# A one-core hybrid decoder layer: products of ones where TensorE waits, a fixed order of the first loads, new FFN shares and leads, one half's sums inside the last down products

## The chip, the cores and the metric

The kernel runs on one core of one Trainium2 chip. The metric is device time in microseconds (us) of one execution. Five engines work side by side, each through its own list of instructions in a fixed order: TensorE (PE in the profile; the load of its stationary operand is a row of its own, PEld), VectorE (DVE), ScalarE (ACT), GpSimd (POOL) and SyncE (SP), which here only starts DMA transfers. An engine that waits for a semaphore holds up everything behind it on its list.

## The reference

One layer for 2056 tokens: a prompt of 2048 and 8 decode tokens. Everything is float32.

```
n  = rmsnorm(x, g1);   [x_branch 512 | gate 512 | q 512 | k 128 | v 128] = n @ w_in
rec = lru(conv4(x_branch)) * gelu(gate)              # per-token scan, block-diagonal gates
att = window_attention(q, k, v, sinks)               # 8 heads, self + 128 tokens back
h  = x + concat(rmsnorm(rec), rmsnorm(att)) @ w_out
h2 = rmsnorm(h, g2);   y = h + (silu(h2 @ w_gate) * (h2 @ w_up)) @ w_down      # 1024 -> 2816 -> 1024
return rmsnorm(y, g_final), the k, v and conv windows, the last LRU states
```

## The kernel before

Tokens lie along the free dimension, features on the 128 partitions. A float32 product is made of a rounded part hi and a remainder lo of each operand: three products, w_hi x_hi, w_hi x_lo and w_lo x_hi, replace each one (`mm3`, issued by `mm`, line 358; transposes by `tr`, line 363). So every weight chunk is loaded raw (`raw_...`, line 344), cast on ACT (line 347) and given a remainder on POOL (line 348), and every activation chunk gets hi on ACT (line 387) and lo on DVE (line 388).

**Head phase, 0 to about 691 us.** Four sub-blocks of 520, 512, 512 and 512 tokens. Per sub-block s: `prep` loads x in 8 chunks (`xs`, line 627), makes hi and lo, and sums squares (ACT line 395 or 398, DVE line 399) into `xacc`; TensorE sums that over the partitions (`st_x`), DVE adds the epsilon (line 409), POOL takes the power -1/2 (line 410), TensorE spreads the result over all partitions (`bc_x`, line 358 as all products), ACT copies it out (`rb_x`, line 426). The 14 input units (`ip<s>_<u>`, 48 products of 260 columns in sub-block 0, 24 of 512 after it) need that factor only when DVE evicts them (line 673). Then follow the recurrence's gates (`g`), attention (`s`, `pt`, `o`), a norm over each group (`st_rc`, `bc_rc`, `st_at`, `bc_at`) and the output units (`op`). In this phase a table, `PE_ORDER`, fixes the order of all products, one token per tile and a count; `order_pe` chains them. The other engines' orders come from a scheduler: each step has a planned due time built from constants (`T_...`, `L_...`, `D_...`, `F_...`), and instructions go out by these. Before sub-block 0 stands a chain of small DVE operations on the parameter vector (lines 585 to 604: `hab`, `hxb`, `nsk`, `sp`, `c2`, `nc2`).

**FFN, about 691 to 2060 us.** Three groups gi of about 688 tokens, two halves n each. For each of 11 pairs p of hidden chunks, gate and up come as seven products of sums and differences of quarters (`ps_g`, `ps_u`, numbered r); ACT copies them out (lines 1337, 1342, 1344), DVE and POOL combine them (lines 1298 to 1316). The down product is either plain (`pd`, 16 tiles, added to `y` on DVE at line 1373) or, for gi 1 and 2 and p 1 to 9, again in seven products (`pw`, added at line 1402). Remainders of the weights are made at line 1131 (gate, up) and line 1200 (`wd`, down). Tables `E_...` say for each of these operations whether POOL ("P") or DVE ("V") does it.

**Tail.** `finish` squares each finished `y` chunk of the last group (ACT, line 398), adds the squares on DVE (line 399), then runs `st_f`, the power, `bc_f` and, per chunk, one DVE operation (line 1424) and one output DMA on SP (line 1427). The last down products do half 1 (8 tiles) and then half 0 (8 tiles); the sums of both halves come behind them.

Of the kernel before, what the change touches and what calls it, by code (L numbers as in the profile page):

```python
# [67 lines left out]
E_T2 = ['V', 'P', 'P', 'P']
E_HN = ['P', 'P', 'P', 'P']
# [33 lines left out]
ip0_1_0 ip0_1_1 ip0_12_0 ip0_12_1 ip0_1_0:2 ip0_1_1:2 ip0_12_0:2 ip0_12_1:2 ip0_1_0 ip0_1_1 ip0_12_0 ip0_12_1  # L103
ip0_1_0:2 ip0_1_1:2 ip0_12_0:2 ip0_12_1:2 ip0_1_0 ip0_1_1 ip0_12_0 ip0_12_1 ip0_1_0:2 ip0_1_1:2 ip0_12_0 ip0_1_0
ip0_1_1 ip0_12_0:2 ip0_12_1:3 ip0_1_0:2 ip0_1_1 ip0_1_0 ip0_1_1:2 ip0_12_0:3 ip0_12_1:3 ip0_1_0:3 ip0_1_1:3 ip0_12_0
ip0_1_0:2 ip0_1_1:2 ip0_12_0 ip0_1_0 ip0_1_1 ip0_12_0:4 ip0_12_1:2 ip0_1_0:3 ip0_1_1:3 ip0_12_0:3 ip0_12_1:4
ip0_1_0:2 ip0_1_1:2 ip0_12_0:2 ip0_12_1:5 ip0_9_0:3 st_x0:5 ip0_9_0:21 ip0_9_1:18 bc_x0_0:4 ip0_9_1:6 ip0_8_0:24
ip0_8_1:4 bc_x0_4 ip0_8_1:20 ip0_0_0:24 ip0_0_1:19 g0_1_0_0 ip0_0_1:5 ip0_3_0:20 g0_1_0_260 ip0_3_0:4 ip0_3_1:12
g0_1_1_0 ip0_3_1:12 ip0_11_0:14 g0_1_1_260 ip0_11_0:10 ip0_11_1:15 vt0_0 ip0_11_1:9 ip0_10_0:23 vt0_1 ip0_10_0
ip0_10_1:24 ip0_13_0:3 vt0_2 ip0_13_0:21 ip0_13_1:6 vt0_3 ip0_13_1:18 ip0_2_0:7 s0_0_0:4 ip0_2_0:5 s0_0_1:4 g0_0_0_0  # L110
ip0_2_0:12 ip0_2_1:6 s0_1_0:4 s0_1_1:4 ip0_2_1:2 g0_0_0_260 ip0_2_1:10 pt0_0_1:4 ip0_2_1:4 s1_0_0:4 ip0_2_1:2
ip0_5_0:3 s1_0_1:4 ip0_5_0 g0_0_1_0 ip0_5_0:9 o0_0_0 ip0_5_0:10 s1_1_0:4 ip0_5_0 o0_0_0 pt0_1_1:4 ip0_5_1:4
g0_0_1_260 ip0_5_1 s1_1_1:4 ip0_5_1:19 ip0_4_0:2 s2_0_0:4 ip0_4_0:7 o0_1_0 ip0_4_0:11 pt1_0_0:4 o0_1_0 ip0_4_0:2
s2_0_1:4 ip0_4_0:2 ip0_4_1:24 ip1_8_0:15 ip0_6_0:9 o1_0_0 ip0_6_0 pt1_0_1 o1_0_0 pt1_0_1:3 ip0_6_0 ip1_8_0 g0_3_0_0
# [3 lines left out]
s3_0_0:4 ip0_7_0:2 o1_1_1:2 s3_0_1:4 bc_x1_0 ip0_7_1:2 bc_x1_0 ip0_7_1:3 pt2_0_0:4 ip0_7_1:19 o2_0_0:2 pt2_0_1:2  # L118
g0_2_0_0 pt2_0_1 ip1_10_0:8 pt2_0_1 ip1_10_0:12 o2_0_1 ip1_10_0 g0_2_0_260 ip1_10_0 s3_1_0:4 pt2_1_0:4 s3_1_1:4
ip1_10_0:2 o2_0_1 ip1_11_0:14 g0_2_1_0 ip1_11_0:10 ip1_4_0:4 o2_1_0 ip1_4_0:2 pt2_1_1 o2_1_0 pt2_1_1:3 g0_2_1_260  # L120
ip1_4_0:18 ip1_0_0:2 o2_1_1 ip1_0_0 vt1_0 ip1_0_0:6 dS:2 o2_1_1 dS:6 pt3_0_0:4 ip1_0_0:12 o3_0_0 ip1_0_0:3
ip1_12_0:2 dS2:2 ip1_12_0:2 pt3_0_1 o3_0_0 ip1_12_0 pt3_0_1:3 ip1_12_0:18 o3_0_1 ip1_12_0 ip1_13_0:4 o3_0_1
pt3_1_0:4 ip1_13_0:9 dS3 ip1_13_0 dS3 ip1_13_0:10 ip1_1_0 o3_1_0 pt3_1_1:3 ip1_1_0:2 pt3_1_1 o3_1_0 ip1_1_0 dS4:4
s4_0_0 dS4:4 ip1_1_0:8 o3_1_1 s4_0_0:3 s4_0_1:4 ip1_1_0:2 o3_1_1 ip1_1_0:10 ip1_5_0:7 dS5:2 s4_1_0:2 s4_1_1:4
ip1_5_0 s4_1_0:2 vt1_1 ip1_5_0:11 pt4_0_0:2 ip1_5_0 pt4_0_0:2 ip1_5_0:4 s5_0_0:4 ip1_2_0 s5_0_1:4 ip1_2_0 vt1_2
ip1_2_0:7 o4_0_0 ip1_2_0:9 pt4_0_1 o4_0_0 pt4_0_1:3 ip1_2_0:3 vt1_3 ip1_2_0:3 o4_0_1 s5_1_0:4 s5_1_1:4 o4_0_1
pt4_1_0:4 st_rc0:5 ip1_6_0:24 pt4_1_1:4 bc_rc0_0:3 s6_0_0:4 bc_rc0_0 s6_0_1:3 pt5_0_0:4 bc_rc0_4 s6_0_1 g1_0_0_0
g1_0_1_0 st_at0:5 ip1_3_0:24 bc_at0_0:4 ip1_7_0:24 op0_0_0:2 bc_at0_4 op0_0_0:10 op0_0_260:12 op0_1_0 g1_1_0_0
op0_1_0:11 op0_0_0 op0_0_260 op0_1_0:4 op0_0_0:6 op0_1_0:3 op0_0_260:9 op0_1_0:3 op0_0_0:3 g1_1_1_0 op0_0_0:2
op0_0_260:2 op0_1_0:2 o4_1_0:2 op0_1_260:4 o4_1_1:2 op0_1_260:20 op0_2_0:11 pt5_0_1:4 op0_2_0:12 o5_0_0:2 op0_2_0  # L130
op0_2_260:13 s6_1_0:4 op0_2_260:3 s6_1_1:4 op0_2_260:2 o5_0_1 op0_2_260:6 op0_3_0:5 o5_0_1 g1_2_0_0 op0_3_0
pt5_1_0:4 op0_3_0:18 op0_3_260:16 g1_2_1_0 op0_3_260:8 op0_4_0:18 o5_1_0 op0_4_0:2 pt5_1_1 o5_1_0 op0_4_0 pt5_1_1:3
op0_4_0:3 op0_4_260:24 op0_5_0 o5_1_1 s7_0_0:4 op0_5_0:4 s7_0_1:4 op0_5_0:8 o5_1_1 pt6_0_0:4 op0_5_0:11 op0_5_260:11
g1_3_0_0 op0_5_260:13 o6_0_0 op0_6_0:3 pt6_0_1 o6_0_0 pt6_0_1:3 op0_6_0:5 g1_3_1_0 op0_6_0:10 o6_0_1 op0_6_0:6
op0_6_260 s7_1_0:4 op0_6_260 s7_1_1:4 op0_6_260 o6_0_1 pt6_1_0:4 op0_6_260:21 op0_7_0:17 o6_1_0 bc_x2_0:3 pt6_1_1
o6_1_0 bc_x2_0 pt6_1_1:3 op0_7_0:7 op0_7_260:17 o6_1_1 op0_7_260:7 ip2_4_0:20 o6_1_1 pt7_0_0:4 ip2_4_0:4 ip2_0_0:8
st_h0:5 ip2_0_0:2 o7_0_0 ip2_0_0:2 o7_0_0 ip2_0_0:6 pt7_0_1:4 ip2_0_0:6 ip2_5_0:2 st_rc1:4 o7_0_1 ip2_5_0:3 o7_0_1
pt7_1_0:4 ip2_5_0:13 bc_rc1_0:4 ip2_5_0:3 o7_1_0 ip2_5_0:3 pt7_1_1:3 ip2_1_0:2 pt7_1_1 o7_1_0 ip2_1_0:8 g2_0_0_0
ip2_1_0:12 o7_1_1 ip2_1_0:2 o7_1_1 g2_0_1_0 ip2_8_0:24 ip2_12_0:18 g2_1_0_0 ip2_12_0:6 ip2_9_0:19 g2_1_1_0 ip2_9_0:5
ip2_10_0:24 ip2_11_0:3 vt2_0 ip2_11_0:21 ip2_2_0:8 vt2_1 ip2_2_0:16 ip2_13_0:6 vt2_2 ip2_13_0:18 ip2_7_0:7 vt2_3  # L140
ip2_7_0:17 ip2_3_0:5 s8_0_0:4 s8_0_1:3 st_at1:4 s8_0_1 ip2_3_0:19 ip2_6_0 s8_1_0:4 s8_1_1 bc_at1_0:4 s8_1_1
# [1425 lines left out]
```

## Time and profile before

| What | Before |
|---|---|
| Runs | 2077.74, 2079.32, 2082.77 us; median 2079.32 us |
| Profiled execution | 2078.05 us, of which the span is 2076.3 us |
| Around the span | 1.75 us |
| Mean granted TensorE clock | 0.994 of full |
| PE / DVE / ACT / POOL busy | 2014.0 / 1440.0 / 939.9 / 929.3 us |
| DMA | 450.96 MB, mean 217 GB/s |

Times in the profile's rows count from the start of the span. In a timeline row stand start, duration, engine, line, operation, output tile and operands, partitions x elements, count; in brackets how long the engine had been idle, and what ended that. A row of windows gives, for a stretch, its length and for each engine its busy time and instructions, then the granted clock (1.00 is full), the DMA share and GB/s. The list of waits gives total, number and longest. A float32 product that is not split leaves two records.

### The profile page before, as it was taken

The page shows a single profiled execution, that of the slowest core. Times are in us where ns is not written, and L with a number is a line of the kernel's source. Part 1 is how long each engine was busy: PE and PEld are TensorE (multiplying, and loading weights), DVE is VectorE, ACT ScalarE, POOL GpSimd, SP SyncE. Part 2 cuts the span into 40 slices and gives each one's busy share as a digit, 9 for nine tenths or more (in the row PEclk, how much of TensorE's full clock was granted, in tenths as well). Part 3 has the DMA queues.
Part 4 walks back from the last instruction along what each step waited for, and adds up shares of the span by engine and source line. Part 5 has one row for each costly group of instructions (what it writes and reads, how often), then busy time and mean ns, then how long its engine had stood idle before and what let it go on. Part 6 is the DMA issues. An engine that isn't in the chain of part 4 may idle for free.

```text
span 2076.3 us, 34690 instructions
## 1 busy us (share of the span) xinstructions
PE 2014.0 (97%) x12238; PEld 1903.0 (92%) x12238; DVE 1440.0 (69%) x2683; ACT 939.9 (45%) x1954; POOL 929.3 (45%) x820
## 2 busy tenths in 40 slices
PE   8999899999999999999999999999999999999997
PEld 8988787878777899999999999999999999999997
DVE  6786896766885755656654578777666666777676
ACT  5764684563554543344334533334335433433342
POOL 5212342020122787667776845455446522433332
PEclk9999999999999999999999999999999999999998
DMA  8864485576677955656555776776677775566652
GB/s 300 264 209 149 165 281 178 189 241 198 205 259 263 332 200 199 211 201 215 189 197 187 253 266 213 244 235 227 217 242 251 241 231 195 183 197 196 195 181 87
DMA packets 208990, 450.96 MB, mean 217 GB/s; under 512 B 25232, under 2 KB 82720, under 8 KB 208800
## 3 DMA queue, kind: packets, MB, share of 16 engines
q1 hardware_dynamic: 205616, 446.24, 64.4%
q10 hardware_dynamic: 3200, 2.51, 0.4%
q8 instruction: 96, 1.57, 0.3%
q14 instruction: 78, 0.64, 0.1%
HBM read 335.89 MB, written 113.84 MB: 217 GB/s over the span
## 4 chain that ended last, share of the span: by engine, by line
PE 69%; DVE 12%; DMA 9%; issue 4%; ACT 3%; POOL 2%; SPq 1%; DVEq 0%; ACTq 0%; POOLq 0%
PE ps_u L358 17%; PE ps_g L358 17%; PE pd L358 10%; PE ip L358 10%; PE pw L358 9%; DMA n<-hs 4%; PE op L358 2%; DMA rd<-in_wdown 1%; DMA xs<-in_xT 1%; DMA mixed<-n 1%; DVE y L1424 1%; DVE xc L696 1%; DVE n L485 1%; DVE n L477 1%; PE o L358 1%
## 5 line engine op out<-in xcount | busy, mean ns | idle before, releaser
L358 PE MATMUL ps_g<-hn,w_g 128*128 128x342 f32 (+1 forms) x2772 | 491.9, 321 | 4.7 <-ACT c_g L1337 2.5
L358 PE MATMUL ps_u<-hn,w_u 128*128 128x342 f32 (+1 forms) x2772 | 482.5, 320 | 0.7 <-ACT c_u L1342 0.7
L358 PEld LDWEIGHTS ps_g<-hn,w_g 128*128 128x128 f32 x2772 | 447.0, 189 | 6.4 <-ACT c_g L1337 2.7
L358 PEld LDWEIGHTS ps_u<-hn,w_u 128*128 128x128 f32 x2772 | 444.3, 189 | 1.6 <-ACT c_u L1342 1.0
L358 PE MATMUL ip<-xn,w_in 128*128 128x512 f32 (+1 forms) x1680 | 354.3, 360 | 11.7 <-ACT xn L387 8.3
L358 PEld LDWEIGHTS ip<-xn,w_in 128*128 128x128 f32 x1680 | 274.2, 192 | 57.1 <-ACT xn L387 8.3
L1402 DVE TENSOR_TENSOR y<-y,pw 128x342 f32<-128x342 f32 x504 | 238.6, 503 | 55.4 <-PE pw L358 54.2
L358 PE MATMUL pd<-fh,w_d 128*128 128x344 f32 (+1 forms) x960 | 238.7, 321 | 1.5 <-DVE y L1373 1.5
L358 PE MATMUL op<-mix,w_out 128*128 128x512 f32 (+1 forms) x960 | 205.1, 359 | 1.5 <-ACT mix L777 1.4
L358 PEld LDWEIGHTS op<-mix,w_out 128*128 128x128 f32 x960 | 156.2, 189 | 30.5 <-issue 5.3
L358 PE MATMUL pw<-fh,wd 128*128 128x342 f32 x576 | 168.2, 321 | 2.5 <-DVE y L1402 2.5
L358 PEld LDWEIGHTS pd<-fh,w_d 128*128 128x128 f32 x960 | 168.2, 188 | 2.1 <-DVE y L1373 1.8
L1373 DVE TENSOR_TENSOR y<-y,pd 128x344 f32<-128x344 f32 (+1 forms) x240 | 117.0, 506 | 70.6 <-PE pd L358 69.1
L1298 POOL TENSOR_TENSOR c_u<-c_u,c_g 128x342 f32<-128x342 f32 (+1 forms) x60 | 63.7, 1062 | 210.3 <-DVE c_u L1316 199.4
L1287 DVE TENSOR_TENSOR fl<-c_u,fh 128x342 fp32r<-128x342 f32 (+1 forms) x132 | 115.6, 882 | 59.9 <-ACT fh L1286 58.4
L358 PE MATMUL pd<-fl,w_d 128*128 128x344 f32 (+1 forms) x480 | 154.0, 321 | 1.6 <-DVE fl L1287 1.6
L1286 ACT CAST fh<-c_u 128x342 fp32r<-128x342 f32 (+1 forms) x132 | 62.5, 479 | 161.1 <-POOL c_u L1298 87.7
L1200 POOL TENSOR_TENSOR wd<-rd,wd 128x512 fp32r<-128x512 f32 x72 | 98.5, 1369 | 77.9 <-ACT wd L1199 75.0
L358 PE MATMUL pw<-t,wd 128*128 128x342 f32 x648 | 125.1, 320 | 3.7 <-DVE y L1402 3.7
L1316 DVE TENSOR_TENSOR c_u<-c_u,ps_u 128x342 f32<-128x342 f32 (+1 forms) x99 | 50.3, 508 | 107.0 <-PE ps_u L358 106.7
L1130 ACT CAST w_u<-ru 128x512 fp32r<-128x512 f32 x99 | 61.3, 620 | 111.0 <-PE pd L358 38.0
L358 PEld LDWEIGHTS pw<-t,wd 128*128 128x128 f32 x648 | 105.8, 189 | 5.3 <-DVE y L1402 4.9
(280 smaller groups left out, 3479.6 us busy)
## 6 DMA issues: line engine op xcount, KB each, us to landing
w_g<-split_g SPq DMA_DIRECT2D x88, 512.0 KB, 4.4
w_u<-split_u SPq DMA_DIRECT2D x88, 512.0 KB, 5.3
w_in<-split_w SPq DMA_DIRECT2D x84, 512.0 KB, 3.8
rg<-in_wgate SPq DMA_DIRECT2D x110, 256.0 KB, 3.3
ru<-in_wup SPq DMA_DIRECT2D x110, 256.0 KB, 3.3
w_out<-split_w SPq DMA_DIRECT2D x48, 512.0 KB, 5.1
split_g<-w_g SPq DMA_DIRECT2D x44, 512.0 KB, 3.6
split_u<-w_u SPq DMA_DIRECT2D x44, 512.0 KB, 3.7
```

Of the source, the lines that this page charges most:

```text
L358: r = nc.tensor.matmul(*args, **kw)
L477: nc.vector.scalar_tensor_tensor(x, x, col(V_G2 + k), bc[n][:, :nn], ALU.mult, ALU.mult)
L485: (nc.gpsimd if M_MIX else nc.vector).tensor_tensor(x, a, b, op=op)
L696: nc.vector.scalar_tensor_tensor(xc[:, :n], xr[:, j:j + n], cw[j], xc[:, :n], ALU.mult, ALU.add)
L1130: nc.scalar.copy(w[:, 0, :], src)
L1200: eng((E_DLO1, E_DLO2)[gi - 1][j]).tensor_tensor(w[:, :, 1], v, w[:, :, 0].bitcast(F32), op=ALU.subtract)
L1286: nc.scalar.copy(hi, v)
L1287: nc.vector.tensor_tensor(lo, v, hi.bitcast(F32), ALU.subtract)
L1298: (nc.vector if p == NPAIR - 1 or src is not v else eng(E_MUL[2 * h + n])).tensor_tensor(v, src, g, op=ALU.mult)
L1316: nc.vector.tensor_tensor(o, a, b, op)
L1373: nc.vector.tensor_tensor(ys[gi, n, m], ys[gi, n, m], ps, ALU.add)
L1402: nc.vector.tensor_tensor(v, v, ps, ALU.add)
```

## The change

It has four parts.

**1. Products of ones.** `PE_ORDER` now also holds tokens `w_<tile>:n`. When that tile is allocated, n products of a 128x128 block of ones with itself go into its first 128 columns; the tile's own first product overwrites them (`start=True`). They wait for whatever the tile's memory waits for, and for nothing else. There are 48: st_x0 9, pt2_0_0 2, bc_rc0_4 1, st_at0 6, o8_0 1, s11_1_1 1, pt15_0_0 1, op3_0_0 4, op3_3_1 1, ps_g0_0_5 13, and in the tail st_f2_0 5 and bc_f2_0 4.

```
+        def filled(ps, name):
+            for _ in range(FILLS["w_" + name]):
+                mm("w_" + name, ps[:, :P], ones, ones, start=True, stop=True)
+            return ps
```

**2. First loads.** `prep(0)` is replaced by `prep_first`, which issues the first weights and x chunks in one list, chains ACT's casts, hi parts and squares in the same order, and chains DVE's lo parts (0 to 7) and square additions (8 + chunk):

```
+FIRST = [(1, 0), 0, (12, 0), 1, 2, 3, (1, 1), 4, 5, (12, 1), 6, 7, -1]
+FIRST_DVE = [0, 1, 9, 2, 3, 10, 4, 5, 6, 7, 11, 12, 13, 14, 15]
```

A pair (u, i) is half i of the weights of unit u, a number an x chunk, -1 the constants `cs`, which ACT's queue loaded before. On SP's queue the first rows were these (`raw_in_u_i` is a weight half, `xs` an x chunk, the last two share a tile):

```order
L344 DMA raw_in_1_0_278<-in_win 128x512
L344 DMA raw_in_1_1_284<-in_win 128x512
L344 DMA raw_in_12_0_290<-in_win 128x512
L627 DMA xs_0_195<-in_xT 128x520
L627 DMA xs_1_202<-in_xT 128x520
L627 DMA xs_2_210<-in_xT 128x520
L627 DMA xs_3_218<-in_xT 128x520
L344 DMA raw_in_12_1_296<-in_win 128x512
```

and now they are:

```order
L351 DMA raw_in_1_0_159<-in_win 128x512
L671 DMA xs_0_162<-in_xT 128x520
L351 DMA raw_in_12_0_164<-in_win 128x512
L671 DMA xs_1_167<-in_xT 128x520
L671 DMA xs_2_169<-in_xT 128x520
L671 DMA xs_3_171<-in_xT 128x520
L351 DMA raw_in_1_1_173<-in_win 128x512
L671 DMA xs_4_176<-in_xT 128x520
```

The first x chunk has moved from fourth to second place. On DVE the 31 small operations of the parameter chain, which stood ahead of the first lo part and among the following ones, now stand behind the last square addition.

**3. Shares, leads, order.** Planner constants and the recorded `PE_ORDER` have new values; for the most part products swap places with a neighbour. Of the shares these change (what moves is counted from the engines' lists):

```
-E_LO0 = ['P', 'V', 'P', 'V', 'P', 'V', 'P']      +E_LO0 = ['V', 'V', 'V', 'V', 'P', 'P', 'P']
-E_LO2 = ['V', 'V', 'V']                          +E_LO2 = ['V', 'V', 'P']
-E_DLO1 = ['P', 'V', 'P', 'V', 'V', 'P', 'V']     +E_DLO1 = ['P', 'P', 'P', 'V', 'P', 'V', 'V']
-E_DLO2 = ['P', 'P', 'P', 'P', 'P', 'P', 'V']     +E_DLO2 = ['V', 'P', 'V', 'P', 'V', 'V', 'P']
-E_T1 = ['P', 'P', 'P', 'V']                      +E_T1 = ['P', 'P', 'P', 'P']
-E_T2 = ['V', 'P', 'P', 'P']                      +E_T2 = ['P', 'V', 'P', 'P']
-E_HN = ['P', 'P', 'P', 'P']                      +E_HN = ['P', 'V', 'P', 'P']
```

Group 0: 22 remainders of gate and up go from POOL to DVE. Group 1: 9 remainders `wd` and 9 combinations `c_u` go from DVE to POOL, 7 `hn` from POOL to DVE. Group 2: 22 remainders of gate and up go from DVE to POOL, 27 `wd` and 7 `hn` from POOL to DVE.

At the start of the FFN, TensorE's list (`ps_g_0_r` is product r of the gate of pair 0; number 6 takes the memory of number 1, number 5 that of an earlier output unit) had

```order
L358 MATMUL ps_g_0_2_7775<-hn_0_4_6445,w_g_0_2_7723 128x344
L358 MATMUL ps_g_0_1_7758<-hn_0_5_6452,w_g_0_6_7738 128x344 x3
L358 MATMUL ps_g_0_1_7758<-hn_0_6_6512,w_g_0_6_7738 128x344 x4
L358 MATMUL ps_g_0_1_7758<-hn_0_7_6532,w_g_0_6_7738 128x344
L358 MATMUL ps_g_0_1_7758<-hn_0_6_6512,w_g_0_6_7738 128x344
L358 MATMUL ps_g_0_1_7758<-hn_0_7_6532,w_g_0_6_7738 128x344 x3
L358 MATMUL ps_g_0_5_7809<-hn_1_0_7638,w_g_0_5_7742 128x344 x4
```

and now has

```order
L384 MATMUL ps_g_0_2_7803<-hn_0_4_6461,w_g_0_2_7751 128x344
L384 MATMUL ps_g_0_5_7837<-ones 128x128 x13
L384 MATMUL ps_g_0_5_7837<-hn_1_0_7666,w_g_0_5_7770 128x344 x4
L384 MATMUL ps_g_0_5_7837<-hn_1_1_7679,w_g_0_5_7770 128x344
L384 MATMUL ps_g_0_5_7837<-hn_1_0_7666,w_g_0_5_7770 128x344
L384 MATMUL ps_g_0_5_7837<-hn_1_1_7679,w_g_0_5_7770 128x344 x3
L384 MATMUL ps_g_0_5_7837<-hn_1_2_7688,w_g_0_5_7770 128x344 x3
L384 MATMUL ps_g_0_1_7786<-hn_0_5_6472,w_g_0_6_7766 128x344 x3
```

Products 5 and 6 have changed places, and 13 products of ones stand ahead of number 5.

**4. Tail.** `finish_last` replaces `finish` for the last group. Half 1's squares are added on DVE (odd chunks) and POOL (even), half 0's on POOL, and half 0's last square is not added but summed by TensorE. Half 1's last DVE operations run from the first on as its factor comes, those from the third on behind half 0's last `y` addition and those from the sixth on behind half 0's epsilon addition. Half 0's output DMAs alternate between SP's and ACT's queue.

```
+F_PLACE = [3, 6]
+F_HOLD = [2, 5]
+            for place, r in zip(F_PLACE, ends):
+                for m in range(place, KD):
+                    behind(tail_pd[m], r)
```

Behind the last down product (`pd_10_7_0`) TensorE's list ended with

```order
L358 MATMUL pd_10_7_0_22494<-fh_10_10_7627,w_d_10_11_22327 128x342
L358 MATMUL st_f_1_22506<-avg,acc_f_1_22346 114x1 x3
L358 MATMUL st_f_0_22520<-avg,acc_f_0_22434 114x1 x3
L358 MATMUL bc_f_1_0_22512<-cs,cols_f_1_22417 128x114 x3
L358 MATMUL bc_f_0_0_22530<-cs,cols_f_0_22505 128x114 x3
```

and now ends with

```order
L384 MATMUL pd_10_7_0_22548<-fh_10_10_7655,w_d_10_11_22368 128x342
L384 MATMUL st_f_0_22564<-ones 128x128 x5
L384 MATMUL st_f_0_22564<-avg,acc_f_0_7486 114x1
L384 MATMUL st_f_0_22564<-avg,sq_f_0_7_22561 114x1
L384 MATMUL st_f_0_22564<-avg,acc_f_0_7486 114x1
L384 MATMUL st_f_0_22564<-avg,sq_f_0_7_22561 114x1
L384 MATMUL st_f_0_22564<-avg,acc_f_0_7486 114x1
L384 MATMUL st_f_0_22564<-avg,sq_f_0_7_22561 114x1
L384 MATMUL bc_f_0_22578<-ones 128x128 x4
L384 MATMUL bc_f_0_22578<-cs,cols_f_0_22563 128x114 x3
```

Half 1's two groups of small products (`st_f_1`, `bc_f_1`) have left this place; they now stand ahead of tiles 3 and 6 (counted from 0) of half 0's eight down tiles.

More of the change, by code (lines that the diff above doesn't have):

```diff
@@ L108 @@
[L108 to L112, printed above, removed]
```

433 lines of the change are left out of this document (272 added, 161 removed).

## The prediction

> **What bounds the kernel now.** I read the page first, then the waits of TensorE, then windows of 3.41 us, then the timelines of the start and the end. On the page TensorE is busy nearly throughout:
>
> ```profile
> PE 2014.0 (97%) x12238; PEld 1903.0 (92%) x12238; DVE 1440.0 (69%) x2683; ACT 939.9 (45%) x1954; POOL 929.3 (45%) x820
> ```
>
> So the time is the sum of TensorE's products plus what it loses in between: 2076.3 - 2014.0 = 62 us idle, and some products at a lower clock. The change adds 48 products and removes none, so whatever it gains comes out of these losses. The waits of TensorE name them (total, number, longest):
>
> ```profile
> PE ip L358 <- ACT xn L387: 8.3, 1, 8.3
> PE pw L358 <- DVE y L1402: 6.3, 8, 1.9
> ...
> PE st_at L358 <- ACT ia L711: 1.7, 1, 1.7
> ...
> PE op L358 <- ACT mix L777: 1.4, 1, 1.4
> ```
>
> The largest is the first: 8.3 us until the first product can run. The rest are small and many. The clock is the second kind of loss. It sits at half only in single stretches; these windows show them, the loss ahead and, for two, the half clock behind it:
>
> ```profile
> 217.11:220.53 3.42, 1.89 (x14) 1.69 (x15) 3.39 (x6) 3.21 (x6) 0.00 (x0) 1.00 0.00 0
> 220.53:223.94 3.41, 3.41 (x10) 2.67 (x9) 3.41 (x7) 1.38 (x2) 1.73 (x1) 0.50 0.00 0
> 544.79:548.21 3.42, 1.53 (x7) 0.74 (x5) 3.42 (x13) 2.41 (x8) 2.04 (x3) 1.00 0.45 116
> ...
> 636.95:640.37 3.42, 2.03 (x12) 1.77 (x13) 3.42 (x6) 3.23 (x6) 0.00 (x0) 1.00 0.75 260
> ...
> 694.98:698.39 3.41, 0.96 (x6) 0.88 (x6) 3.38 (x6) 2.24 (x5) 2.83 (x2) 1.00 0.99 324
> 698.39:701.81 3.42, 3.42 (x14) 3.42 (x13) 3.42 (x4) 1.90 (x2) 2.65 (x3) 0.50 1.05 403
> ...
> 1507.34:1510.76 3.42, 1.60 (x10) 1.60 (x11) 2.65 (x7) 0.00 (x0) 0.00 (x0) 1.00 1.03 394
> ```
>
> Where TensorE was busy for 0.96 to 2.03 us of a window, the clock (third number from the end) was 0.50 in the next one (220.53 and 698.39 show it); the window of 1.60 at 1507 was followed by none, so the bound isn't sharp. Each drop costs up to half of 3.41 us, 1.7 us. A product of ones therefore has a purpose where it lifts a window above the bound, and a price where it stands behind the wait.
>
> **Price of a product of ones.** It isn't in the trace. The nearest rows are the broadcasts of one 128x128 float32 block:
>
> ```profile
> 634.51 1.16 PE L358 MATMUL bc_rc<-cs,rccols 128*128 128x128 f32 x8 [0.34 <-POOL rccols L410]
> 635.43 0.47 PE L358 MATMUL o<-pth,vt 128*128 128x512 f32 x1
> ```
>
> Eight records are four products; from 634.51 to the next start they took 0.92 us, so 0.23 us each at full clock, 0.46 at half.
>
> **Start.** Up to the norm's sums (`st_x`) everything hangs on the first loads and on DVE:
>
> ```profile
> 8.26 1.24 PE L358 MATMUL ip<-xn,w_in 128*128 128x260 f32 x4 [8.26 <-ACT xn L387]
> ...
> 24.69 1.08 PE L358 MATMUL st_x<-avg,xacc 128*104 128x1 f32 x10
> ```
> ```profile
> 4.12 0.62 ACT L347 CAST w_in<-raw_in 128x512 fp32r<-128x512 f32 x1 [0.96 <-DMA raw_in<-in_win]
> 7.48 0.73 ACT L387 ACTIVATE xn<-xs,vec 128x520 fp32r<-128x520 f32 x1 [0.16 <-DMA xs<-in_xT]
> ```
> ```profile
> 16.45 1.30 POOL L348 TENSOR_TENSOR w_in<-raw_in,w_in 128x512 fp32r<-128x512 f32 x1 [2.63 <-DMA split_w<-w_in]
> 16.47 1.31 DVE L599 TENSOR_SCALAR sp<-sp 128x4 f32<-128x4 f32 x1
> 21.21 0.75 DVE L388 SCALAR_TENSOR_TENSOR xn<-xs,vec,xn 128x520 fp32r<-128x520 f32 x1
> 21.88 0.21 DVE L698 SCALAR_TENSOR_TENSOR xc<-scv,vec,xc 128x8 f32<-128x8 f32 x1
> 22.02 0.15 DVE L603 TENSOR_SCALAR c<-sp 128x4 f32<-128x4 f32 x1
> 23.95 0.69 DVE L399 TENSOR_TENSOR xacc<-xacc,sq_x 128x520 f32<-128x520 f32 x1
> 31.98 0.43 DVE L673 TENSOR_TENSOR xr<-ip,rb_x 128x260 f32<-128x260 f32 x1 [6.01 <-ACT rb_x L426]
> ```
>
> The first weight landed at 4.12, the first x chunk, three loads later, at about 7.4: 1.1 us a load. Second in the queue it lands near 5.2, its hi part takes 0.73, so the first product runs at about 5.9 instead of 8.26. From there DVE decides. It makes eight lo parts (0.75 each, 6.0 us) and seven additions (0.69 each, 4.8); and it stands still while POOL makes a weight remainder, as the pair at 16.45 and 16.47 shows (1.31 us for an operation that takes 0.15 otherwise). Four such remainders fall into this stretch, 1.2 us each, 4.8 us. That is 15.6 us, less the 0.08 us by which one starts before the one ahead ends (0.75 at 21.21, the next at 21.88) at each of 15, about 14.5; from 5.9 the last addition ends near 20.5 instead of 24.64. So `st_x` comes 4.2 us earlier. The 96 products ahead of it have by then been issued either way. The nine products of ones (4.1 us at half clock) lie in the time when TensorE waits for the first load and cost nothing there.
>
> What is late next: the 31 small DVE operations, now behind the last addition. At 0.15 each they need 4.7 us, and the idle time they move into is 6.01 us, ahead of the first eviction. POOL's remainders may stretch them by 1 to 2 us beyond it, and TensorE itself then stands about 2.5 us ahead of `st_x`, long enough for a drop. I take 0.7 us off: **3.5 us gained, bounds 5.5 and 1.0**.
>
> **Head phase after it.** At 640 the four products of ones (0.9 us) lie in the 1.4 us wait of `op`, so they cost nothing and lift that window to 2.9: 1.7 gained. At 218 the six stand behind the release that `st_at` waits for (1.7 us) and cost 1.4 us; the drop they prevent costs 1.7: 0.3 gained. At 548 no product of ones stands near; the order there changes a little, and I take 0.6 of the possible 1.7. The swaps of neighbours in the order I can't price; the nearest rows are the single waits above, 1.4 to 1.9 us, so two of them either way. **2.6 gained, bounds 6 gained and 3 lost.**
>
> **Start of the FFN.**
>
> ```profile
> 691.14 3.92 PE L358 MATMUL ps_g<-hn,w_g 128*128 128x344 f32 x24
> 697.52 5.59 PE L358 MATMUL ps_g<-hn,w_g 128*128 128x344 f32 x24 [2.45 <-ACT c_g L1337]
> ```
>
> The second 24 products waited for ACT's copy of product 1, whose memory product 6 takes, and then ran half cold: 5.59 against 3.92, 1.67 us lost. Now product 5 comes first, whose memory is free; but 13 products of ones (3.0 us) stand ahead, from 695.06 to 698.05, so real work starts 0.5 us later, at full clock. Ahead of them nothing queues on TensorE that could have gone; behind them the whole list. **1.2 gained; bounds 2.5 gained, or 1.5 lost** if the second half's `hn`, which ACT and DVE make just then, isn't ready at 698.
>
> **Shares in the FFN.**
>
> ```profile
> 1138.00:1582.00 444.00, 435.08 (x2761) 430.86 (x2761) 317.73 (x564) 168.94 (x352) 237.05 (x218) 1.00 0.70 235
> 1595.00:2025.00 430.00, 429.09 (x2738) 428.51 (x2737) 303.47 (x541) 168.07 (x349) 162.81 (x140) 1.00 0.64 206
> 691.00:1120.00 429.00, 422.32 (x2666) 420.04 (x2665) 255.77 (x381) 174.88 (x349) 317.83 (x238) 1.00 0.61 209
> ```
> ```profile
> L1200 DVE TENSOR_TENSOR wd<-rd,wd 128x512 fp32r<-128x512 f32 x18 | 17.0, 945 | 0.0
> ...
> L1312 DVE TENSOR_TENSOR c_u<-c_u,c_u 128x342 f32<-128x342 f32 x9 | 5.1, 563 | 0.0
> ```
> ```profile
> L1131 POOL TENSOR_TENSOR w_g<-rg,w_g 128x512 fp32r<-128x512 f32 x21 | 30.3, 1442 | 21.4 <-ACT w_g L1130 18.6 <-DMA sums_d<-sd 1.5 <-issue 1.3
> ...
> L1200 POOL TENSOR_TENSOR wd<-rd,wd 128x512 fp32r<-128x512 f32 x18 | 25.1, 1397 | 22.4 <-ACT wd L1199 22.4
> ```
>
> TensorE idles 444.0 - 435.1 = 8.9 us in group 1, 0.9 in group 2, 6.7 in group 0 (2.45 of it priced above). In group 1 DVE gives away 9 x 0.945 + 9 x 0.563 = 13.6 us and takes seven `hn`, so it falls from 318 to about 311 us of 444. The 6.3 us for late `y` additions are all DVE's; I give a quarter back, 1.5. In group 0 POOL, the fullest engine at 318 of 429, loses 22 x 1.44 = 32 us: 0.5. In group 2 DVE loses 22 remainders and gains 27 `wd` at 0.945 and seven `hn`, about even, and there is nothing to win: 0. **2.0 gained, bounds 8 gained and 6 lost** (all idle time of groups 0 and 1 above gone by half, or group 2 taking on group 1's 6.3).
>
> **Tail.**
>
> ```profile
> 2060.03 0.51 DVE L1373 TENSOR_TENSOR y<-y,pd 128x342 f32<-128x342 f32 x1
> ...
> 2060.64 0.49 ACT L398 ACTIVATE sq_f<-y 128x342 f32<-128x342 f32 x1 [0.45 <-DVE y L1373]
> ...
> 2061.83 0.73 PE L358 MATMUL st_f<-avg,acc_f 128*114 128x1 f32 x6 [1.33 <-DVE acc_f L399]
> 2062.42 0.90 PE L358 MATMUL bc_f<-cs,cols_f 114*128 114x114 f32 x6
> ...
> 2062.84 0.85 POOL L410 TENSOR_TENSOR cols_f<-cols_f,nhalf 114x3 f32<-114x3 f32 x1 [0.86 <-DVE cols_f L409]
> 2063.36 7.78 DVE L1424 SCALAR_TENSOR_TENSOR y<-y,vec,bc_f 128x342 f32<-128x342 f32 x16 [0.60 <-PE bc_f L358]
> ```
>
> All 16 last DVE operations (7.78 us, 0.486 each) ran behind the first `bc_f`; the last ends at 2071.14. Half 1's sums and broadcast, about 0.6 and 0.75 us, now stand between the down products, so these end 1.3 us later and the last `y` addition ends at 2061.84. Then: square 0.49, to 2062.4; `st_f` 0.7, to 2063.2; epsilon and power, to 2064.5 (1.1 from the end of `st_f` to that of POOL, as at 2062.56 to 2063.69, plus 0.2); `bc_f` 0.9 to 1.6, to 2065.7; eight operations, 3.9, to 2069.6. Half 1's eight fit into the time before it. **1.5 gained, bounds 2.5 gained and 1 lost** (if half 0's additions on POOL, some 0.85 each, fall behind a `y` every 0.94 us).
>
> **Sum.** 3.5 + 2.6 + 1.2 + 2.0 + 1.5 = 10.8 us. The profiled execution took 2078.05 us, 1.27 under the median of 2079.32; the sum goes off the median: 2079.32 - 10.8 = 2068.5 us.
>
> **Rivals.** (1) The front gains don't reach the end: what follows is timed by transfers, and the drops come elsewhere, since a shifted stream meets other windows (the window at 1507 escaped, another may not). Then start and head give nothing: 1.2 + 2.0 + 1.5, 2074.6 us. For it: waits such as the 2.03 us window at 636 come from attention and the mix, whose DVE and ACT work is not made less. Against: the loads of sub-block 0 start earlier too. (2) The products of ones don't do what they are for. If only an unbroken idle stretch as long as a window lowered the clock, none of the inner drops would be due to the waits, the longest of which inside the kernel is 2.45 us; the products of ones would only cost: 1.4 at 218, 0.5 at 695. Sum: 3.5 - 1.4 - 0.5 + 2.0 + 1.5 = 5.1, 2074.2 us. The four windows ahead of drops speak against it, the window at 1507 for it. [...] (3) Slower: in group 2 `wd` now falls on DVE as often as in group 1 before, and every `y` addition queued behind it releases `pw` late. Group 1's eight waits averaged 0.8 us, the longest 1.9; one per pair at 1.35 us over 18 pairs is 24 us, so 2079.32 - 10.8 + 24 = 2092.5. It decides from 17 us on, 0.95 us a pair. Against it: group 1's DVE was at 72% and lost only 6.3 in all.
>
> **How the numbers follow.** Forecast 50% (about 2062 to 2073), a larger gain 10%, rival 1 22%, rival 2 8%, rival 3 10%. A measurement of this kernel can tell about 0.3%, 6.2 us, from no change, so faster means below 2073.1. The forecast nearly whole, the larger gain and a twentieth of rival 1 make 0.63; rivals 1 and 2 mostly lie within: 0.27; slower 0.10. The range of 8 in 10 leaves out half of the larger gains and rival 3: 2060 to 2079.
>
> **What would show it.** In the changed trace: the first product of `ip` near 5.9 and `st_x` near 20.5; `bc_x` and the first eviction earlier by the same; no window at 0.50 near 216, 636 and 694; no wait of `ps_g` for `c_g`; waits of `pw` for `y` below 6 us, none in group 2; the last output operation about 11 us earlier. Wrong would make it: `st_x` early but the first `g` not, new half-clock windows, or `pw` waiting in group 2.

## The result, and the profile after

The changed kernel took 2071.16 us (median of five, 2069.34 to 2071.59); before took 2082.77 us beside it (2077.74 to 2087.0). The ratio is 0.9944, 95% interval 0.9925 to 0.9964: 11.6 us faster, against a forecast of 10.8. The time itself is 2.6 us above the 2068.5 that was named: the median it was taken from, 2079.32, was that of three runs, and two further runs of before beside the changed kernel were slower. Beside the experiments before lay between 2077.6 and 2093.3 us, with medians of 2084.3 to 2086.8, so differences of two profiles are read with care below.

On the page TensorE is busy longer in a shorter span, 2022.7 of 2069.8 us. Of the waits, the first is gone, and `pw` waits for `y` 3.5 us instead of 6.3:

```profile
PE 2022.7 (98%) x12340; PEld 1911.6 (92%) x12340; DVE 1461.3 (71%) x2703; ACT 941.7 (45%) x1954; POOL 908.1 (44%) x799
```
```profile
PE pw L384 <- DVE y L1472: 3.5, 3, 2.0
...
PE ip L384 <- DVE xr L739: 2.0, 1, 2.0
...
PE st_at L384 <- ACT ia L777: 1.7, 1, 1.7
...
PE ps_g L384 <- DVE xres L1109: 1.4, 1, 1.4
```

Where the time went is seen by stage. Two traces of each kernel (the second ones are the runs e0 and e8 below), in us; a group ends with the start of its last `y` addition:

| Stage | before | before again | changed | changed again |
|---|---|---|---|---|
| to the first `ps_g` | 691.1 | 695.8 | 690.7 | 688.9 |
| group 0 | 475.5 | 475.7 | 473.8 | 472.3 |
| group 1 | 459.1 | 461.0 | 457.7 | 456.9 |
| group 2 | 434.2 | 434.2 | 433.9 | 433.9 |
| to the end of the span | 16.2 | 16.3 | 13.8 | 13.2 |

**The start** of the changed kernel on TensorE, then (shown for comparison) three rows of before:

```profile
1.05 4.21 PE L384 MATMUL st_x<-ones 128*128 128x128 f32 x18 [1.05 <-DVE carry L578]
5.86 0.50 PE L384 MATMUL ip<-xn,w_in 128*128 128x260 f32 x2 [0.60 <-ACT xn L413]
...
21.01 1.08 PE L384 MATMUL st_x<-avg,xacc 128*104 128x1 f32 x10
...
26.57 1.03 PE L384 MATMUL bc_x<-cs,xcols 104*128 104x104 f32 x8
27.38 3.82 PE L384 MATMUL ip<-xn,w_in 128*128 128x260 f32 x30
33.16 0.75 PE L384 MATMUL ip<-xn,w_in 128*128 128x260 f32 x4 [1.96 <-DVE xr L739]
...
41.52 0.60 PE L384 MATMUL g<-xc,gw 128*128 128x260 f32 x2
...
233.38 0.40 PE L384 MATMUL op<-mix,w_out 128*128 128x260 f32 x2
```
```profile
30.37 1.04 PE L358 MATMUL bc_x<-cs,xcols 104*128 104x104 f32 x8
...
43.07 0.60 PE L358 MATMUL g<-xc,gw 128*128 128x260 f32 x2
...
233.38 0.40 PE L358 MATMUL op<-mix,w_out 128*128 128x260 f32 x2
```

The first product came at 5.86 and `st_x` at 21.01, 3.7 us ahead of before. `bc_x` is 3.8 ahead, the first `g` 1.6, and the first output unit, at 233.38, not at all. DVE shows the first place where the lead is spent (the last row is the first eviction, which came at 31.98 in before):

```profile
20.87 0.16 DVE L611 TENSOR_SCALAR hab<-vec 128x4 f32<-128x4 f32 x1
...
23.26 3.41 DVE L621 TENSOR_TENSOR sp<-sp 128x4 f32<-128x4 f32 x1
...
32.62 0.16 DVE L630 TENSOR_SCALAR nc<-sp 128x4 f32<-128x4 f32 x1
32.69 0.42 DVE L739 TENSOR_TENSOR xr<-ip,rb_x 128x260 f32<-128x260 f32 x1
```

The moved parameter chain runs from 20.87 to 32.8, 11.9 us. Of its 31 operations 27 take 0.16 to 0.18 us each, three 1.1 to 1.2 and one 3.41; most of the rest is the 0.20 us from the start of one to that of the next, which needs its result. The first eviction waits for the chain and comes 0.7 us later than in before, and TensorE waits for the eviction.

**The clock.** These windows of the changed kernel are the counterpart of those shown of before:

```profile
5.26:8.67 3.41, 2.02 (x12) 1.61 (x13) 2.04 (x2) 3.37 (x7) 2.32 (x2) 1.00 1.01 347
8.67:12.08 3.41, 3.41 (x18) 3.41 (x18) 3.41 (x5) 3.41 (x7) 1.37 (x1) 0.50 1.05 402
...
694.98:698.39 3.41, 2.40 (x21) 2.40 (x22) 3.41 (x5) 1.48 (x4) 2.85 (x2) 1.00 1.00 334
...
1254.54:1257.95 3.41, 1.40 (x10) 1.12 (x9) 3.38 (x6) 0.00 (x0) 1.11 (x1) 1.00 0.88 332
1257.95:1261.36 3.41, 3.41 (x14) 3.41 (x14) 2.89 (x7) 1.14 (x2) 0.49 (x1) 0.50 0.92 289
```

The four half-clock windows of before are gone; two others have come, one at the start and one at 1258, in each case behind a window with 1.40 to 2.02 us of work. Each of these six stretches at a clock of 0.50 lasted 3.41 to 3.42 us, the length of the windows here and in the prediction. (In both kernels the clock is at 0.50 in the last microseconds too, from 2063.7 on in before and from 2060.1 here; that stretch counts in the mean clock.)

**The start of the FFN.** The products of ones did not start at once:

```profile
690.65 3.92 PE L384 MATMUL ps_g<-hn,w_g 128*128 128x344 f32 x24
696.00 3.17 PE L384 MATMUL ps_g<-ones 128*128 128x128 f32 x26 [1.42 <-DVE xres L1109]
698.92 4.04 PE L384 MATMUL ps_g<-hn,w_g 128*128 128x344 f32 x24
```

They waited 1.42 us for DVE to empty the memory that product 5 takes over.

**The tail:**

```profile
2056.03 0.51 DVE L1441 TENSOR_TENSOR y<-y,pd 128x342 f32<-128x342 f32 x1 [0.43 <-PE pd L384]
...
2059.84 1.43 PE L384 MATMUL bc_f<-cs,cols_f 114*128 114x114 f32 x6 [0.19 <-POOL cols_f L1529]
2061.38 3.94 DVE L1540 SCALAR_TENSOR_TENSOR y<-y,vec,bc_f 128x342 f32<-128x342 f32 x8 [1.09 <-PE bc_f L384]
```

Eight operations instead of 16 stand behind the last broadcast. From the last `y` addition to the end it takes 13.8 us instead of 16.2.

### The profile page after: what moved, and what is told of

Same layout as the page of the kernel before. It is cut to its first block, busy times and chain, and to the rows that moved or that the text cites. A ratio compares the mean times of both kernels' runs of the same rounds, so it can differ in the third digit from the quotient of the medians.

```text
span 2069.8 us, 34896 instructions
## 1 busy us (share of the span) xinstructions
PE 2022.7 (98%) x12340; PEld 1911.6 (92%) x12340; DVE 1461.3 (71%) x2703; ACT 941.7 (45%) x1954; POOL 908.1 (44%) x799
## 4 chain that ended last, share of the span: by engine, by line
PE 73%; DVE 11%; DMA 7%; ACT 4%; issue 3%; POOL 1%; SPq 0%; DVEq 0%; POOLq 0%; ACTq 0%
PE ps_g L384 18%; PE ps_u L384 18%; PE pd L384 11%; PE pw L384 10%; PE ip L384 9%; PE op L384 3%; DMA n<-hs 3%; DMA xt<-in_xR 1%; DVE xc L762 1%; DMA hn<-mixed 1%; DMA xs<-in_xT 1%; PE o L384 1%; PE pt L389 1%; DMA m<-mixed 1%; ACT sc L945 1%
## 5 line engine op out<-in xcount | busy, mean ns | idle before, releaser
L1353 DVE TENSOR_TENSOR fl<-c_u,fh 128x342 fp32r<-128x342 f32 (+1 forms) x132 | 108.6, 827 | 46.8 <-ACT fh L1352 46.5
L1197 POOL TENSOR_TENSOR w_u<-ru,w_u 128x512 fp32r<-128x512 f32 x44 | 59.3, 1347 | 180.1 <-ACT w_u L1196 158.2
L384 PEld LDWEIGHTS pw<-fh,wd 128*128 128x128 f32 x576 | 106.2, 190 | 1.5 <-DVE y L1472 1.4
```

The lines of the kernel that those rows point to most:

```text
L384: r = nc.tensor.matmul(*args, **kw)
L1197: lo_eng.tensor_tensor(w[:, 1, :], src, w[:, 0, :].bitcast(F32), op=ALU.subtract)
L1353: nc.vector.tensor_tensor(lo, v, hi.bitcast(F32), ALU.subtract)
```

## The experiments

Twelve kernels ran, each beside runs of before on the same chip; a ratio is to those, with its 95% interval. Two theories stand against each other: roughly, A is that a part gains through what the forecast gave for it, B that its gain is lost at the next wait or was never there; each expectation says it for its run. With six to twelve runs each, a difference of less than about 5 us between two of these kernels is not separated by the intervals; where a text below decides on less, it does so by the traces.

**e0: before again.** No edit.

> The kernel of before, unchanged, as a run of its own, because its five times lie between 2077.7 and 2087.0 us while those of the changed kernel lie within 2.3 us. Theory A, the spread is the clock: windows near the bound fall now below it, now above, so slow executions of this kernel show a lower mean clock (0.994 at 2078; about 0.990 at 2087, since a mean lower by 0.001 is 2 us of half work) and the profile another set of half-clock windows. Theory B, the spread comes from transfers or queues: the mean clock stays at 0.993 to 0.995 in all of them. Ratio to before 1.000 either way.

Ratio 0.9997 (0.9983 to 1.0011), times from 2078.7 to 2091.6 us. Over these 12 and the 17 runs beside them the clock and the time go together only loosely: the five with a mean clock of 0.991 average 2089.8 us, the five with 0.994 2083.2, but those with 0.993 reach from 2078.7 to 2090.6. So the clock may be a part of the spread, and theory A alone doesn't explain it. Half-clock windows stood at 221.6, 644.8, 702.9 and 1515.2 in this trace; against the first trace of before the one at 548 has gone and the one at 1515 has come. So the places of the half-clock windows differ between two executions of the same kernel.

**e1, e2: without products of ones.** e1 strips all 48 `w_` tokens, e2 leaves the nine at the start.

```
-w_st_x0:9 ip0_1_0 ...   w_st_at0:6 st_at0:5 ...   w_ps_g0_0_5:13 g0_0_5:12 ...
+ip0_1_0 ...             st_at0:5 ...              g0_0_5:12 ...
-FILLS.update({"w_st_f2_0": 5, "w_bc_f2_0": 4})
```

> The changed kernel without any of the 48 products of ones. Theory A, they hold the clock: half-clock windows return at about 220 and 698, perhaps at 640, 1.7 us each, against 1.4 and 3.0 us of their own time saved at 218 and 696; the start runs half cold until 12 to 15 us, which DVE hides. About 1 us slower than the changed kernel, 2072 us, with a larger spread. Theory B, an idle window does not lower the clock: 3 to 5 us faster than the changed kernel, 2066 to 2068 us. If the ones at the start matter, st_x comes later than 21.0 us.

> The changed kernel with the nine products of ones at the start and none of the other 39. Theory A: as without any, half-clock windows near 220 and 698, 2072 us; st_x stays at 21.0. Theory B: 3 to 5 us faster than the changed kernel. The difference to the run without any is what the nine at the start are worth: 0 if DVE hides the cold start, up to 2 us if it does not.

e1: 2071.84 us, ratio 0.9930 (0.9912 to 0.9948). e2: 2074.36 us, 0.9944 (0.9925 to 0.9962). The changed kernel itself, measured again as e8: 0.9935 (0.9919 to 0.9951). All three are the same within their intervals: theory B's 3 to 5 us don't show, and theory A's 1 us is less than these runs can tell. `st_x` came at 20.98 without any product of ones and at 21.01 with the nine, so those at the start don't matter to it. In the 3.41 us from 8.67 on e1 ran 25 records, where the changed kernel ran 18 at a clock of 0.50; so its start was not, as its expectation has it, at half clock until 12 us or later. Half-clock windows did return in e1:

```profile
218.30:221.70 3.40, 2.83 (x13) 2.64 (x14) 3.40 (x7) 3.05 (x6) 0.00 (x0) 0.50 0.00 0
221.70:225.13 3.43, 3.43 (x10) 2.66 (x9) 3.40 (x7) 1.18 (x2) 1.54 (x1) 0.50 0.01 2
...
641.55:645.00 3.45, 3.45 (x14) 3.11 (x13) 3.45 (x7) 0.75 (x2) 0.00 (x0) 0.50 0.19 56
...
713.23:716.65 3.42, 3.42 (x15) 3.42 (x13) 1.42 (x1) 0.75 (x3) 3.34 (x4) 0.50 0.93 327
```

The first two rows are one stretch at half clock, 6.8 us long. All fourteen traces together say how far the ones hold the clock. Near 220 us each of the seven traces without the six ones has a half-clock window, and of the seven with them only that of e4, where the ones themselves ran at half clock (2.93 us for the six, 1.60 or 1.61 in the other traces). At 640 to 645, and again at 698 to 713, five of the seven traces without ones at that place have one, but e2 and e11 have none at either; of the seven with them e7 alone has one, at 698.7. And others come where no ones stand: e8, the changed kernel, has four, at 7.8, 76.0, 253.5 and 1253.6. So theory A holds for the clock at 220 and is less sure at the other two places; what a higher clock saves in time isn't shown by e1 and e2.

At the start of the FFN, e2 shows what the 13 ones cost:

```profile
688.52 3.92 PE L384 MATMUL ps_g<-hn,w_g 128*128 128x344 f32 x24
692.99 4.03 PE L384 MATMUL ps_g<-hn,w_g 128*128 128x344 f32 x24 [0.55 <-DVE xres L1109]
```

Product 5 starts 0.55 us behind the first 24 records here, and 4.35 us behind them in the changed kernel. Yet group 0 takes 473.8 us in both, so the 3.8 us are taken back further on; which wait takes them was not singled out.

**e3: old shares.** The eight tables of before in the changed kernel: the seven of the diff above, backwards, and `E_DSUM`, of whose eight entries the one "V" had moved from the sixth to the last place.

> The changed kernel with the eight tables of shares (E_LO0, E_LO2, E_DLO1, E_DLO2, E_DSUM, E_T1, E_T2, E_HN) of before. If the shares made the gain within the FFN (4.3 us in group 0 by the two traces, about 0 in group 1, 0.7 in group 2), 3 to 5 us slower than the changed kernel, 2075 us, most of it lost between 720 and 1120 us. If leads and order made it: 2070 to 2072 us.

2074.1 us, ratio 0.9943 (0.9926 to 0.9960); between the two expectations, about 2 us behind e8 in its ratio and level with the changed kernel's first one (0.9944), which the intervals don't separate. In its trace group 0 took 475.5 us, as before, and group 2 435.7 instead of 433.9. So the changed kernel keeps nearly all of its gain, about 12 us, without any of the new shares.

**e4: parameter chain later.**

```
-                yield T_PRO
+                yield 30.0
```

> The changed kernel with the 31 small operations of the parameter chain given a due time of 30 us, so that DVE does the first seven evictions ahead of them. In the changed kernel's trace TensorE waited 1.96 us for the first eviction at 31.2 us, since DVE was still in that chain. Theory A, the chain takes back half of the front gain: that wait goes, the second bc_x moves from 33.75 to about 31.8. If nothing else holds the stream, 2 us faster than the changed kernel. Theory B, attention and the gates set the pace up to 110 us anyway: the gain is gone there as well and the time stays within 0.5 us.

2070.36 us, ratio 0.9937 (0.9919 to 0.9954), against 0.9935 of the changed kernel: theory B, by the trace more than by the time. The wait went, the second `bc_x` came at 31.50 and the first `g` 2 us earlier still, yet the first output unit is no earlier than in before, 233.38:

```profile
39.49 0.68 PE L384 MATMUL g<-xc,gw 128*128 128x260 f32 x2
...
234.95 0.40 PE L384 MATMUL op<-mix,w_out 128*128 128x260 f32 x2
```

**e5: first loads alone.** Before with `prep_first`, `split_load`, `split_raw`, `FIRST`, `FIRST_DVE` and the late chain; nothing else.

> The kernel of before with the new first loads alone (order of the loads, of ACT and of DVE at the start, parameter chain behind the sums), no products of ones, all else as before. Theory A, the front gain reaches the end: 3 to 4 us faster than before. Theory B, read from the two traces, where the lead of 3.9 us at st_x was 1.6 at 35 us and 0 at 102 us: bc_x about 3 us earlier, but the outputs of the first sub-block at 233 us within 0.5 us of before, and the time within 1 us.

2083.68 us, ratio 0.9994 (0.9981 to 1.0007): theory B again, though 3.5 us, a ratio of 0.9983, still lies just within the interval. `bc_x` came 2.3 us earlier than in before, the first output unit later:

```profile
28.07 1.03 PE L370 MATMUL bc_x<-cs,xcols 104*128 104x104 f32 x8
...
234.16 0.40 PE L370 MATMUL op<-mix,w_out 128*128 128x260 f32 x2
```

**e7: products of ones alone.** Before with `filled` and four tokens: `w_st_x0:9`, `w_st_at0:6`, `w_op3_0_0:4`, and `w_ps_g0_0_5:13` ahead of `g0_0_6`.

> The kernel of before with the four large groups of products of ones (9 ahead of the first product, 6 at st_at0, 4 at op3_0_0, 13 at the start of the FFN ahead of the product that waits), all else as before. Theory A, they hold the clock and narrow the spread: no half-clock windows near 220, 640 and 700, 5.1 us saved and 1.9 paid, so 3 us faster than before, with a spread below the 13 us of before. Theory B, they only cost: 0 to 2 us slower.

2088.48 us, ratio 1.0024 (1.0009 to 1.0038): 5 us slower (1.9 to 7.9), more than theory B gave. The trace shows why at one place, the start of the FFN (last two rows): the memory wasn't free, and the ones started late and at half clock (0.50 from 698.70 to 705.50).

```profile
219.74 1.61 PE L367 MATMUL st_at<-ones 128*128 128x128 f32 x12 [1.73 <-ACT ia L720]
...
691.92 3.92 PE L367 MATMUL ps_g<-hn,w_g 128*128 128x344 f32 x24
699.49 5.92 PE L367 MATMUL ps_g<-ones 128*128 128x128 f32 x26 [3.65 <-DVE xres L1052]
```

The drop there came anyway, the 3.0 us became 5.9, and real work began only at 705. Group 0 took 479.7 us in this trace, 4 us more than in the two of before, so this one place is most of the loss. At 220 and at 640 no drop came, as priced; e7 doesn't tell what the ones at these two places are worth by themselves.

**e8: the changed kernel again.**

> The changed kernel itself, on the same chip and beside the same runs of before as the others of this call, since the kernel of before has shown medians from 2079.3 to 2086.8 us. If its time holds from call to call: 2070 to 2072 us, spread 3 us, and a ratio of 0.993 to 0.995.

2071.11 us, 2065.6 to 2075.2, ratio 0.9935 (0.9919 to 0.9951). The narrow spread of its first five runs, 2.3 us, did not hold: it is 9.6 here.

**e6: half 1's broadcast behind the last tile.**

```
-F_PLACE = [3, 6]
+F_PLACE = [8, 8]
```

> The changed kernel with half 1's broadcast no longer held ahead of the last down tiles (F_PLACE 8, 8: the broadcast goes behind the last tile, the statistics product stays where the scheduler puts it). Theory A, the placement makes the tail's gain (2.5 to 3 us from the last y addition to the end in the traces): half 1's eight last operations start about 2.5 us later and crowd with half 0's, 1 to 2 us slower than the changed kernel, with the stretch behind the last y addition back at 15 us or more. Theory B, the gain is half 0's shorter chain alone: same time within 0.5 us.

2071.25 us, ratio 0.9934 (0.9917 to 0.9952): theory B. The broadcast ran at 2054.88, behind the last tile, and the last eight operations still began 5.2 us after the start of the last `y` addition (5.3 in the changed kernel). The whole tail of the change is still in this kernel; only the place of the broadcast is tried:

```profile
2054.88 0.82 PE L384 MATMUL bc_f<-cs,cols_f 114*128 114x114 f32 x6
2055.08 0.51 DVE L1441 TENSOR_TENSOR y<-y,pd 128x342 f32<-128x342 f32 x1 [0.43 <-PE pd L384]
...
2060.33 3.94 DVE L1540 SCALAR_TENSOR_TENSOR y<-y,vec,bc_f 128x342 f32<-128x342 f32 x8 [0.58 <-PE bc_f L384]
```

**e9: one table alone.** Before with

```
-E_LO0 = ['P', 'V', 'P', 'V', 'P', 'V', 'P']
+E_LO0 = ['V', 'V', 'V', 'V', 'P', 'P', 'P']
```

> The kernel of before with one table changed, E_LO0 (22 remainders of group 0's weights from POOL to DVE). Theory A, POOL held group 0 up: from the first product of the FFN to the last y addition of group 0 about 474 us instead of 476 to 477, 2 to 3 us faster than before. Theory B, the shares only pay together with the leads: within 1 us of before.

2075.78 us against 2085.27, ratio 0.9963 (0.9948 to 0.9977): 7.7 us, more than theory A gave, from a single line. Groups 0 and 1 in windows, of before, of this kernel and of the changed one:

```profile
733.00:1130.00 397.00, 393.93 (x2501) 392.79 (x2501) 231.10 (x357) 153.63 (x305) 286.34 (x215) 1.00 0.58 200
1130.00:1590.00 460.00, 451.08 (x2863) 446.86 (x2862) 325.67 (x578) 176.62 (x369) 244.90 (x225) 1.00 0.71 235
```
```profile
733.00:1130.00 397.00, 397.00 (x2527) 397.00 (x2527) 249.88 (x379) 155.60 (x309) 264.76 (x198) 1.00 0.58 201
```
```profile
733.00:1130.00 397.00, 396.90 (x2525) 396.61 (x2524) 247.30 (x380) 156.15 (x310) 263.99 (x196) 1.00 0.58 201
1130.00:1590.00 460.00, 452.44 (x2864) 448.58 (x2863) 330.17 (x570) 179.86 (x375) 263.04 (x238) 1.00 0.72 238
```

POOL falls from 286 to 265 us, DVE rises from 231 to 250, and TensorE's idle time in this stretch of group 0 goes from 3.1 us to none. From its first product to its last `y` addition group 0 takes 473.8 us, 1.7 and 1.9 us less than in the two traces of before, which is what theory A said of it. The other 6 us can't be found in this trace: its execution took 2077.96 us, as long as the profiled one of before, and its other stages lie within the spread of before. Nor does the run tell whether POOL's smaller load or the new order of the entries does it, since the edit changes both.

**e10: old planner numbers of the FFN.** The changed kernel with the old lines of `U_M`, `U_D`, `U_R`, `L_RW`, `F_LEAD`, `F_HN`, `F_FIN`, `F_MIX`, `F_DOWN`.

> The changed kernel with the old planner numbers of the FFN (U_M, U_D, U_R, the L_RW line, F_LEAD, F_HN, F_FIN, F_MIX, F_DOWN), all else, shares too, as changed. Theory A, the leads made group 1's gain (459 to 465 us before, 455 to 458 after, and 458 with the old shares): group 1 back at 460 us or more, 3 to 6 us slower than the changed kernel, about 2076 us. Theory B, shares and order do it: 2070 to 2072 us.

2070.8 us, ratio 0.9935 (0.9917 to 0.9953): theory B, the numbers are worth nothing that can be measured. Group 1 took 458.9 us, not the 460 or more of theory A.

**e11: the smallest set.** No products of ones, and of the shares only `E_LO0` new.

> The changed kernel without products of ones and with the new share of group 0 alone (the tables of groups 1 and 2 as before): the smallest set of shares that the traces bear out. If the shares of groups 1 and 2 and the ones are worth nothing, 2070 to 2072 us, a ratio of 0.993; if the shares of group 1 count, 2 us more.

2069.12 us, ratio 0.9930 (0.9910 to 0.9950). It has the lowest median of all, yet its interval holds that of the changed kernel; it does as well with 48 products and seven changed tables less, and isn't shown to be faster.

## Why the prediction was right, and where it was not

The total came out: 11.6 us (ratio 0.9944, 0.9925 to 0.9964) against 10.8. The terms did not all, so that the sum fits is in good part luck. The stages of all fourteen traces show where time was gained, in us:

| Stage | on the kernel of before (before, e0, e5, e7, e9) | on the changed kernel (the other nine) |
|---|---|---|
| to the first `ps_g` | 691.1 to 695.8 | 688.5 to 694.5 |
| group 0, old `E_LO0` | 475.5 to 476.5, e7 479.7 | 475.5 (e3) |
| group 0, new `E_LO0` | 473.8 (e9) | 472.3 to 474.2 |
| group 1 | 459.1 to 464.9 | 453.5 to 458.9 |
| group 2 | 434.2 to 434.3 | 433.2 to 435.7 |
| to the end of the span | 15.9 to 16.3 | 13.0 to 13.9 |

- **Start, 3.5 us: failed.** The times up to the sums were right (5.86 for 5.9, 21.0 for 20.5). That DVE stands still for the whole of a POOL remainder, 4.8 us for four, was an estimate from one pair of rows; in the changed trace, with five remainders beside them, the eight lo parts took 1.09 us in the mean and the seven additions 0.85, in all 3.8 us more than at 0.75 and 0.69 each. Two steps failed. The first is "I take 0.7 us off": the chain of small operations was given 4.7 us and 1 to 2 more, and took 11.9, so the first eviction, forecast to come earlier by as much as `bc_x`, came 0.7 us later than in before. The second is that a lead there counts at the end: with that wait out of the way (e4) the first `g` is 3.6 us ahead of before, and the lead is gone by 233 us all the same; e5 finds 0.9994 for the first loads alone. Rival 1 was right for this term. What paces the stretch from 44 to 233 us wasn't singled out; in it TensorE waits 2.0 us for `ra` in the changed trace and 1.3 in before.
- **Head phase, 2.6 us: not shown to come from the ones.** The window at 695 went from 0.96 to 2.40 us of work and no drop followed, but none followed there in e2 and e11 either. e1 and e2 find no gain from the ones that can be measured. Rival 2's sum is nearer, though not for its reason: near 220 the longest wait of TensorE is 1.73 us, half a window, and in the seven traces without the six products the clock fell to 0.50 there. The stage is 3.7 us shorter in the means of the two traces of each kernel, with a spread of 4.7 between the two of before, and over all the traces the ranges overlap: what there is of it must come from the new order or the head's numbers, neither of which was tried apart.
- **Start of the FFN, 1.2 us: failed.** "Whose memory is free" was wrong, by 1.42 us here and 3.65 us in e7. Product 5 began at 698.92, 0.9 us later than forecast. Nor does a later start there move the whole list behind it, as the forecast had it: e2 begins product 5 3.8 us sooner behind the products ahead of it, and group 0 is no shorter.
- **Shares, 2.0 us: right direction, wrong size and wrong group.** I gave POOL's relief in group 0 half a microsecond. In the traces group 0 is about 2 us shorter with the new `E_LO0`, on either kernel, and e9 measures 7.7 us (0.9948 to 0.9977) for that table alone on before. The row was there: POOL busy 318 of 429 us. I weighed it by TensorE's idle time in one trace, 6.7 us, and took away most of that. Group 1, to which I gave most, is shorter in all nine traces on the changed kernel than in any on before, by 2.7 us in the means of the two traces. But not by its tables, as far as the runs show: with the old ones it took 458.1 us in e3 and 453.5 in e11, and in e3 the waits of `pw` for `y` are 4.1 us, nearer to the 3.5 of the changed kernel than to the 6.3 of before. Rival 3 did not come: group 2 is no longer than before, and no `pw` waits in it.
- **Tail, 1.5 us: right by the traces.** The stretch behind the last `y` addition is 2.4 to 3.1 us shorter by the table of two traces each; less the 1.3 that the forecast charges to the down products, 1.1 to 1.8 are left. Half 0's additions on POOL took 0.91 to 0.99 us each, not 0.85. No run takes the new tail back, so its time wasn't measured alone. e6 shows that the place of half 1's broadcast isn't what counts.

One number of the forecast's chances is off: 0.50, 0.10 and a twentieth of 0.22 make 0.61, not 0.63. Nothing else hangs on it.

By the experiments, then, one table is worth 7.7 us on the kernel of before, and the first loads, the products of ones and the planner numbers of the FFN nothing that can be measured. But the gains don't add up: e3, without any of the new tables, is still about 12 us faster than before, so what else was changed reaches nearly the same without that table. By the stages it is group 1, the tail and perhaps the head. The new order of the products, the head's numbers and the new tail were not taken back in any run, so which of them does it stays open.

## What to carry to other kernels

A lead at the front is worth what is left of it at the next stage boundary: follow one late marker, here the first output unit, before counting it. When one helper engine is at three quarters of a stage, try taking work from it first, measure that alone, and then measure it again by taking it back out of the finished kernel: one table gave 7.7 us when put into before, and all eight together cost about 2 us, within the noise, when taken out at the end. Work that is only there to keep the clock up (near 220 us one of the seven traces with the six products has a half-clock window, and all seven without them have) must lie in a wait whose memory is free, and its own time must be set against the drop: in e7 the 13 products waited 3.65 us for their memory and then took 5.92 us at half clock.

## What the runs showed of the hardware that was not expected

- A lower mean clock went with no more lost time than the half work alone would give, and on the changed kernel with less. Within the runs of before (68 with those of e0, compared only with others on the same chip) 0.001 of the mean clock goes with 1.7 us (standard error 0.3), within those of the changed kernel and its variants (48) with 0.9 (0.3); half work would make it 2.1. These are estimates by a straight line, they show no cause, and the mean clock takes in the half-clock end of the span. For a half-clock stretch of 3.41 us half the work is 1.7 us, the prediction's most for a drop, and that is an estimate; the stretches at 218.30 in e1 and 698.70 in e7 lasted 6.8 us, which makes it 3.4. What a drop costs was not measured alone.
- The same kernel's time varied by 13 us from execution to execution (2078.7 to 2091.6 in e0), with mean clocks from 0.991 to 0.995 that go with only part of it.
- A DVE operation on 128x4 elements, 0.16 us otherwise, took 3.41 us at 23.26 in the changed kernel, while POOL ran from 22.96 to 26.66 without a gap of more than 0.1 us; it ended within 0.01 us of the end of POOL's row. The three DVE operations of 1.10 to 1.21 us in the same chain also lie beside POOL's weight remainders, and two of them end within 0.03 us of where POOL's rows end. Not every DVE operation beside POOL was long: the one at 23.07 took 0.16 us beside POOL's row of 22.96, and in before a reciprocal at 6.34 took 0.18 beside three remainders that ran from 5.02 to 8.73. That the one holds up the other wasn't tried apart. POOL's rows:

```profile
21.51 1.28 POOL L357 TENSOR_TENSOR w_in<-raw_in,w_in 128x512 fp32r<-128x512 f32 x1
22.96 1.18 POOL L436 TENSOR_TENSOR xcols<-xcols,nhalf 104x5 f32<-104x5 f32 x1 [0.17 <-DVE xcols L435]
24.11 2.55 POOL L357 TENSOR_TENSOR w_in<-raw_in,w_in 128x512 fp32r<-128x512 f32 x2
28.75 2.54 POOL L357 TENSOR_TENSOR w_in<-raw_in,w_in 128x512 fp32r<-128x512 f32 x2 [2.09 <-ACT w_in L356]
```
